# The norm of the differential heads in a hybrid attention backbone: per-query sums in a small tile, one root, and a spread by TensorE

## Chip, cores and metric

The kernel runs on one core of a Trainium2 chip. Its time is the device time of one execution in microseconds. Before the change three runs gave a median of 1594.83 us (1593.88 to 1594.98).

## The reference

Two layers are computed on 256 latent tokens and 256 context tokens of width 2048. One input projection feeds three groups of heads: MLA (6 heads), windowed attention (SWA, 6 query heads) and differential attention (4 heads). One output projection takes their gated results. The part that the change touches is the norm over the 128 features of each differential head:

```
oc_x = block_sweep(lambda qb: diff_attend(qb, kc_all, vc_all, lam), qc_x)
yc_x = (rms_norm(oc_x, dif_out_gain[l]) * (1.0 - lam_init)).reshape(b, s, DIFF_WIDTH)
...
y_x = jnp.concatenate([ya_x * silu(mla_gate), yb_x * silu(swa_gate), yc_x * silu(dif_gate)], axis=-1) @ w_out[l]
```

So for each query and each head a sum of 128 squares is made, a reciprocal root is taken of it, and the 128 features of that query and head are multiplied by it. In layer 0 this is done for 512 queries (context included), in layer 1, the last, for the 256 latent ones.

## The kernel before

**Projections.** All products are made in single precision from pieces: a weight block is loaded by a DMA on SP's queue (tile raw), rounded by ScalarE to its high part (hi, L237), and the low part is made by VectorE (lo, L238). TensorE then issues three matmuls for each slice of 128 rows and each token tile: L272 (hi), L273 (lo), L274 (hi, with the low part of the tokens).

**Order of the work.** Each layer runs MLA, then the differential heads (`dif`), then the windowed heads (`swa`), then the output projection. `run(main, side, ...)` issues a list of projection matmuls (main) and weaves in other steps (side) by their costs. A scheduler then orders the instructions of each engine, and each engine works through its own list in that order. The main lists of `swa` start while the last steps of `dif` are still under way. `swa` projects queries in two halves (sq0 and sq1, 384 columns each) and then keys and values. When a token tile of a half is done, ScalarE copies it out of PSUM into a tile sqraw (L1059). The copy, the tile p of the attention steps and the rotary tile rp share one ring of six 128x512 buffers, `stg`. On a latent tile the rotary turn is made by two POOL operations (L640, L641 into rp) and two VectorE operations (L642 on sqraw, L643 adds rp). In layer 0 the `swa` run also carries a fill: a 2048-column adaLN product, whose 1 MB weight tiles wada (16 of them) are loaded on SP's queue between the raw loads (L528) and multiplied by TensorE (L537).

**The norm of the differential heads** is in `C(h, s)` of `dif`, once for each head h and each set s of 256 queries: 8 times in layer 0, 4 times in layer 1. The output o lies in PSUM as features by queries. ScalarE squares it (L1210, tile dn), VectorE applies the gain and the gate (L1211, into oT), and TensorE multiplies by a 128x128 block of ones (L1213), so that each of the 128 rows holds the sums of all 256 queries. The root is taken of the whole 128x256 block: two operations of VectorE (L159, L160), then 13 of POOL (L163, and three rounds of L165 to L168), and a POOL multiply (L1215).

**MLA's keys.** For each pair of heads, `rope_k` (POOL, L944, one operation of 128x512 that writes the rotary part of kn) stands in the side list ahead of `nope_k(0)` and `nope_k(2)` (VectorE L946 and ScalarE L949 write the other part). TensorE transposes kn after that (L197). There are six such places.

Of the kernel before, what the change touches and what calls it, by code (L numbers as in the profile page):

```python
# [10 lines left out]
F32 = mybir.dt.float32  # L11
# [3 lines left out]
AF = mybir.ActivationFunctionType  # L15
ALU = mybir.AluOpType
# [3 lines left out]
P = 128  # L20
# [16 lines left out]
C_ONE = 128  # L37
# [76 lines left out]
class Builder:  # L114
# [36 lines left out]
    def bank_t(self):  # L151
        return self.psx.tile([P, 512], F32, tag="x", name="x")

    def rsqrt(self, y, ss, scale, tmp=None, pool=False):

        v = self.nc.vector
        n = y.shape[-1]
        x, t = tmp if tmp is not None else (self.sm(n, "rx"), self.sm(n, "rt"))
        v.tensor_scalar(x, ss, scale, EPS, ALU.mult, ALU.add)  # L159
        v.tensor_scalar(y.bitcast(I32), x.bitcast(I32), -0.5, 1597463007.0, ALU.mult, ALU.add)  # L160
        if pool:
            v = self.nc.gpsimd
            v.tensor_scalar(x, x, -0.5, 0.0, ALU.mult, ALU.add)  # L163
            for _ in range(3):
                v.tensor_tensor(t, y, y, ALU.mult)  # L165
                v.tensor_tensor(t, t, x, ALU.mult)
                v.tensor_scalar(t, t, 1.0, 1.5, ALU.mult, ALU.add)
                v.tensor_tensor(y, y, t, ALU.mult)  # L168
            return
        v.tensor_scalar(x, x, -0.5, None, ALU.mult)  # L170
        for _ in range(3):
            v.tensor_tensor(t, y, y, ALU.mult)
            v.tensor_tensor(t, t, x, ALU.mult)
            v.scalar_tensor_tensor(y, t, 1.5, y, ALU.add, ALU.mult)
# [179 lines left out]
class Layer:  # L354
# [528 lines left out]
    def mla(self, ip):  # L883
        B, nc, tc = self.B, self.B.nc, self.B.tc
        qt, T = self.qt, self.tok
        nq = len(qt)
# [12 lines left out]
        scale = (P + 64) ** -0.5  # L899
# [3 lines left out]
        for p in range(3):  # L903
# [3 lines left out]
            v = [vv[:, 0], vv[:, 1]]  # L907
# [52 lines left out]
            def nope_k(t):  # L960
                def f():
                    ps = B.bank_t().rearrange("p (h q) -> p h q", h=2)
                    for h in range(2):
                        for i in range(2):
                            B.tr(ps[:, h, i * P:(i + 1) * P], kn[:, t + i, h])
                    B.split(kT[0][:, 0:2, t * P:(t + 2) * P], kT[1][:, 0:2, t * P:(t + 2) * P], ps)
                return f

            def prep_q(s):
                def f():  # L970
                    q = [mp.tile([P, 3, 256], F32R, tag=f"qT{i}", name="qT") for i in range(2)]
                    ql = mp.tile([P, 2, 256], F32R, tag="qTl", name="qTl")
                    qTs[s] = q + [ql]
                    ps = B.bank_t().rearrange("p (h q) -> p h q", h=2)
                    pr = B.bank_t()[:, :256]
                    for i in range(2):
                        for h in range(2):
                            B.tr(ps[:, h, i * P:(i + 1) * P], qr[:, 2 * s + i, h])
                        B.tr(pr[:, i * P:(i + 1) * P], qr[:, 2 * s + i, 2])

                    g = self.prm[:, 73:74]
                    nc.scalar.activation(q[0][:, 0:2], ps, AF.Copy, scale=g)
                    nc.vector.scalar_tensor_tensor(q[1][:, 0:2], ps, g, q[0][:, 0:2].bitcast(F32), ALU.mult, ALU.subtract)
                    B.repeat((q[0][:, 2], q[1][:, 2]), (ql[:, 0], ql[:, 1]), pr)
                return f
# [18 lines left out]
                o = self.pv(lambda k: (v[0][:, 2 * s + k, hh], v[1][:, 2 * s + k, hh]), 4 if s == 0 else 2)  # L1004
                self.gated(h, s, o)
            side = [(300.0, prep_q1, None), (300.0, prep_k1, None)]
            side += [(440.0, f, None) for f in (rope_k, nope_k(0), nope_k(2))]
            pre = {(2 * p, s, 0): [(660.0, prep_q(s), None)] for s in range(nq // 2)}
            side += self.units([(h, s, i) for s in (0, 1) for h in (2 * p, 2 * p + 1) for i in (0, 1)], A, C, pre)
            B.run(gate(p + 1) if p < 2 else [], side, lead=4000.0)  # L1010
# [3 lines left out]
    def swa(self, gp):  # L1014
        B, nc = self.B, self.B.nc
        qt, T = self.qt, self.tok
        nq = len(qt)
# [3 lines left out]
        fill = Fill(self.in_swa, lambda: gp.tile([P, 2048], F32, tag=("skT", "sqT1")[next(turn) % 2], name="wada"), 1) if self.in_swa else None  # L1021
        kT = []
        v = [gp.tile([P, 4, 2, P], F32R, name=f"sv{i}") for i in range(2)]
# [5 lines left out]
        scale = P ** -0.5  # L1029
# [35 lines left out]
        m1 = B.gemm_tok(self.b["sq", 0], nh, nl, NK, qt, 384, ev_q(0))  # L1065
        m2 = B.gemm_tok(self.b["sq", 1], nh, nl, NK, qt, 384, ev_q(1))
        m = m1 + m2 + m0
        B.run(m, fill=(fill, 8, 4, len(m) - 1) if fill else None)

        def prep_q1():  # L1070
            n = 6 * nq
# [5 lines left out]
        def prep_t(g, t):  # L1077
            def f():
                if t == 0:
                    qTs[g] = [gp.tile([P, (3 * T, nT)[i]], F32R, tag=f"sqT{i}", name="sqT")[:, :3 * T].rearrange("p (k t) -> p k t", k=3) for i in range(2)]  # L1080
                ps = B.bank_t().rearrange("p (k q) -> p k q", k=4)[:, :3]
                for i in range(3):
                    B.tr(ps[:, i], qr[g][:, t, i])
                ts_ = slice(t * P, (t + 1) * P)
                B.split(qTs[g][0][:, :, ts_], qTs[g][1][:, :, ts_], ps)
            return f
# [23 lines left out]
        side = self.units([(h, s, i) for h in range(6) for s in (0, 1) for i in (0, 1)], A, C, {(3, 0, 0): [(330.0, prep_t(1, t), None) for t in qt]})  # L1110
        n = len(side) // 3
# [4 lines left out]
    def dif(self, gp):  # L1116
        B, nc = self.B, self.B.nc
        qt, T = self.qt, self.tok
        nq = len(qt)
# [4 lines left out]
        fill = Fill(self.in_dif, lambda: gp.tile([P, 2048], F32, tag=f"dkT{next(turn) % 2}", name="wada"), 1)  # L1124
        kT = []
        v = [gp.tile([P, 4, 512], F32R, name=f"dv{i}") for i in range(2)]
# [4 lines left out]
        scale = 64 ** -0.5  # L1131
# [41 lines left out]
        def prep_q1():  # L1173
            n = 8 * nq
            B.rsqrt(rq[:, 0, :n], ssq[:, :n], 1.0 / 64)
            nc.vector.tensor_scalar(rq[:, 0, :n], rq[:, 0, :n], scale, None, ALU.mult)
            nc.vector.tensor_scalar(rq[:, 1, :n], rq[:, 0, :n], -1.0, None, ALU.mult)
        qTs = {}

        def prep_t(h):  # L1180
            def f():

                qTs[h] = q = [gp.tile([P, T], F32R, tag=f"dqT{i}", name="dqT", bufs=2 - i // 2) for i in range(4)]
                ps = B.bank_t()
                for t in qt:
                    B.tr(ps[:, t * P:(t + 1) * P], qr[:, t, h * P:(h + 1) * P])
                B.repeat(q[:2], q[2:], ps[:, :T])
            return f
# [17 lines left out]
        def C(h, s):  # L1206
            o = self.pv(lambda k: (v[0][:, 2 * s + k, h * P:(h + 1) * P], v[1][:, 2 * s + k, h * P:(h + 1) * P]), 4 if s == 0 else 2)
            d = self.oT[h + 12][:, 256 * s:256 * s + 256]
            x = gp.tile([P, 3, 256], F32, tag="dn", name="dn", bufs=2)
            nc.scalar.activation(x[:, 0], o[:, :256], AF.Square)  # L1210
            nc.vector.scalar_tensor_tensor(d, o[:, :256], self.ogain, d, ALU.mult, ALU.mult)  # L1211
            sv = B.bank_t()
            nc.tensor.matmul(sv[:, :256], B.cst[:, C_ONE:C_ONE + P], x[:, 0], start=True, stop=True)  # L1213
            B.rsqrt(x[:, 0], sv[:, :256], 1.0 / P, (x[:, 1], x[:, 2]), pool=True)
            nc.gpsimd.tensor_tensor(d, d, x[:, 0], ALU.mult)  # L1215

        def gate(p):
            return B.gemm_feat(self.b["dg", p], nh, nl, T, 2, self.gate_fin([12 + 2 * p, 13 + 2 * p]))
        prep_q1()
        prep_t(0)()  # L1220
        B.run(gate(0))
        side = self.units([(h, s, i) for h in range(4) for s in (0, 1) for i in (0, 1)], A, C, {(h, 0, 0): [(440.0, prep_t(h), None)] for h in (1, 2, 3)}, depth=1)
        n = len(side) // 2
        B.run(gate(1), side[:n], lead=2000.0)
        B.run([], side[n:])

    def w_out(self, hp, sink_fn, pools, side=()):

# [182 lines left out]
```

## Time and profile before

| | before |
|---|---|
| median of 3 runs | 1594.83 us |
| profiled execution: its time | 1594.01 us |
| its span | 1592.2 us |
| PE busy | 1523.0 us |
| VectorE (DVE) busy | 921.2 us |
| ScalarE (ACT) busy | 702.3 us |
| POOL busy | 267.8 us |

The span is the time from the first to the last recorded instruction, 1.8 us less than that execution's own time. Busy times are summed over instructions of an engine. A matmul's record overlaps the next one's, so where a stream of matmuls is timed, the distance between starts is what counts. "Clock" is the clock granted to TensorE as a share of 2.4 GHz: 0.50 is 1.2 GHz.

### The profile page before, as it was taken

What the parts mean: (1) busy time and instruction counts of PE and PEld (TensorE: products, weight loads), DVE (VectorE), ACT (ScalarE), POOL (GpSimd) and SP (SyncE); (2) the same over time, 40 slices, a digit from 0 to 9 for tenths busy, and PEclk for the clock granted to TensorE, in tenths of its full rate; (3) what the DMA queues carried; (4) which work ended last, traced back from release to release, by engine and by line L of the source; (5) the groups of instructions that cost most, each with busy time, mean ns of one, the idle gap of its engine ahead of it and who ended that gap; (6) DMA issues with size and microseconds to landing.
All of it is one profiled execution on the core that took longest, in us unless ns stands there. A gap on an engine that the chain in (4) does not pass through costs nothing.

```text
span 1592.2 us, 22493 instructions
## 1 busy us (share of the span) xinstructions
PE 1523.0 (96%) x8213; PEld 1222.9 (77%) x8213; DVE 921.2 (58%) x1922; ACT 702.3 (44%) x1561; POOL 267.8 (17%) x429
## 2 busy tenths in 40 slices
PE   5999999999999987999999999999999999799998
PEld 2667888877778875878887777798876778789887
DVE  3445677642546971345853325958762389638854
ACT  4223556642244651334742224637752356426632
POOL 1002110100111892000010001020100133800100
PEclk9999999999999998999999999999999999999999
DMA  9997312246543125742146667554337662433374
GB/s 334 346 331 201 91 59 60 72 166 231 195 137 95 36 100 199 274 132 80 54 166 220 229 231 259 154 138 138 93 121 253 234 207 82 130 118 120 120 239 144
DMA packets 146769, 262.33 MB, mean 165 GB/s; under 512 B 9531, under 2 KB 90698, under 8 KB 137954
## 3 DMA queue, kind: packets, MB, share of 16 engines
q1 hardware_dynamic: 139056, 246.07, 46.4%
q0 software_dynamic: 2880, 6.39, 1.9%
q10 hardware_dynamic: 4722, 8.43, 1.6%
q8 instruction: 65, 1.06, 0.3%
q14 instruction: 46, 0.38, 0.1%
HBM read 256.63 MB, written 4.22 MB: 164 GB/s over the span
## 4 chain that ended last, share of the span: by engine, by line
PE 48%; DVE 5%; issue 3%; POOL 2%; ACT 2%; DMA 1%; DVEq 0%; POOLq 0%; ACTq 0%
PE g L272 11%; PE g L273 11%; PE g L274 11%; PE x L537 3%; PE x L663 2%; PE g L303 2%; PE g L302 2%; PE g L301 2%; PE x L197 2%; DVE lo L238 2%; ACT hi L237 1%; PE x L706 1%; PE x L707 1%; PE x L708 1%; DMA xres<-in_ctx_dram 0%
## 5 line engine op out<-in xcount | busy, mean ns | idle before, releaser
L238 DVE TENSOR_TENSOR lo<-raw,hi 128x1024 fp32r<-128x1024 f32 (+2 forms) x264 | 313.2, 1188 | 426.6 <-ACT hi L237 421.2
L237 ACT CAST hi<-raw 128x1024 fp32r<-128x1024 f32 (+2 forms) x264 | 266.8, 1011 | 528.9 <-PE g L274 442.8
L273 PE MATMUL g<-lo,nh 128*128 128x512 f32 (+2 forms) x1216 | 460.7, 379 | 14.6 <-DVE lo L238 14.5
L272 PE MATMUL g<-hi,nh 128*128 128x512 f32 (+2 forms) x1216 | 462.7, 382 | 7.6 <-ACT sqraw L1059 5.9
L274 PE MATMUL g<-hi,nl 128*128 128x512 f32 (+2 forms) x1216 | 458.9, 378 | 4.5 <-DVE nl L629 4.5
L272 PEld LDWEIGHTS g<-hi,nh 128*128 128x128 f32 x1216 | 230.6, 190 | 70.4 <-issue 19.3
L273 PEld LDWEIGHTS g<-lo,nh 128*128 128x128 f32 x1216 | 231.2, 190 | 53.7 <-DVE lo L238 17.7
L274 PEld LDWEIGHTS g<-hi,nl 128*128 128x128 f32 x1216 | 230.9, 190 | 45.2 <-DVE nl L629 6.8
L301 PE MATMUL g<-nh,hi 128*128 128x512 f32 (+1 forms) x512 | 175.9, 343 | 0.0
L303 PE MATMUL g<-nh,lo 128*128 128x512 f32 (+1 forms) x512 | 173.4, 339 | 0.0
L302 PE MATMUL g<-nl,hi 128*128 128x512 f32 (+1 forms) x512 | 172.7, 337 | 0.0
L303 PEld LDWEIGHTS g<-nh,lo 128*128 128x128 f32 x512 | 97.0, 189 | 10.2
L301 PEld LDWEIGHTS g<-nh,hi 128*128 128x128 f32 x512 | 97.1, 190 | 9.2 <-DVE v L178 0.4
L302 PEld LDWEIGHTS g<-nl,hi 128*128 128x128 f32 x512 | 97.1, 190 | 9.2
L766 POOL TENSOR_TENSOR oT<-oT,yo 128x256 f32<-128x256 f32 x36 | 28.3, 787 | 333.7 <-ACT yo L764 331.2
L674 DVE TENSOR_REDUCE sst<-x 128x1 f32<-128x512 f32 (+1 forms) x120 | 70.1, 596 | 17.8 <-PE x L663 16.8
L537 PE MATMUL x<-wada,sT 128*32 128x512 f32 x512 | 63.7, 607 | 0.0
L177 ACT CAST pth<-x 128x512 fp32r<-128x512 f32 (+1 forms) x96 | 48.6, 516 | 33.1 <-PE x L197 32.8
L178 DVE TENSOR_TENSOR ptl<-x,pth 128x512 fp32r<-128x512 f32 (+1 forms) x96 | 56.8, 596 | 9.2 <-ACT pth L177 6.0
L197 PE MATMUL x<-cst,p 128*128 128x128 f32 x320 | 51.2, 275 | 3.6 <-DVE p L1203 2.5
L197 PEld LDWEIGHTS x<-cst,p 128*128 128x128 f32 x320 | 37.2, 140 | 15.4 <-issue 6.3
L495 PE MATMUL x<-ar,sT 128*32 128x512 f32 x256 | 35.5, 619 | 11.2 <-DMA ar<-in_w_ada_dram 11.2
(331 smaller groups left out, 2165.2 us busy)
## 6 DMA issues: line engine op xcount, KB each, us to landing
raw<-in_w_in_dram SPq DMA_DIRECT2D x144, 512.0 KB, 3.6
wada<-in_w_ada_dram SPq DMA_DIRECT2D x64, 1024.0 KB, 6.5
raw<-in_w_out_dram SPq DMA_DIRECT2D x72, 512.0 KB, 4.0
ar<-in_w_ada_dram SPq DMA_DIRECT2D x128, 256.0 KB, 6.1
raw<-in_w_in_dram SPq DMA_DIRECT2D x32, 384.0 KB, 3.2
raw<-in_w_in_dram SPq DMA_DIRECT2D x16, 320.0 KB, 3.5
raw<-in_mla_w_uq_dram SPq DMA_DIRECT2D x12, 384.0 KB, 3.1
raw<-in_mla_w_ukv_dram SPq DMA_DIRECT2D x6, 512.0 KB, 3.4
```

What stands on the lines that cost most here:

```text
L178: self.nc.vector.tensor_tensor(lo, src, hi.bitcast(F32), ALU.subtract)
L197: self.nc.tensor.transpose(dst, src, self.ident[:src.shape[0], :src.shape[0]])
L237: nc.scalar.copy(b.hi, raw)
L238: nc.vector.tensor_tensor(b.lo, raw, b.hi.bitcast(F32), ALU.subtract)
L272: mm(ps, xh[:, k, ts_], b.hi[:, kk], start=(i == 0), stop=False)
L273: mm(ps, xh[:, k, ts_], b.lo[:, kk], start=False, stop=False)
L274: mm(ps, xl[:, k, ts_], b.hi[:, kk], start=False, stop=(i == nk - 1))
L301: mm(ps, b.hi[:, kk, fs], xh[:, k, :tok], start=(k == 0), stop=False)
L302: mm(ps, b.hi[:, kk, fs], xl[:, k, :tok], start=False, stop=False)
L303: mm(ps, b.lo[:, kk, fs], xh[:, k, :tok], start=False, stop=(k == NK - 1))
L537: nc.tensor.matmul(st["ps"][32 * j:32 * j + 32], B.sT[:, i, :], st[i][:, 512 * j:512 * j + 512], start=(i == 0), stop=(i == NK - 1), skip_ ...
L674: nc.vector.tensor_reduce(mx, s[:, :n], AX.X, ALU.max)
```

## The change

The change keeps of the norm only the square in `C`. TensorE takes the sum over the features with the squares as the stationary operand and two columns of ones as the moving one, twice for each (h, s), so that the sum of a query lands on its own partition. ScalarE copies one of the columns into a small tile dss of 128 x (tile, head). A new function `dif_norm` takes one root of the whole of dss on VectorE (12 operations of 128x16, in layer 1 of 128x8). Then, for each head, TensorE multiplies a root broadcast over 128 columns by the identity for each tile of tokens, which puts the roots of the queries along the columns on all partitions, and VectorE multiplies the head's oT by that. These five steps are side items of the `swa` run, allowed from its main items 6, 9, 12, 15 and 18 on. The root by POOL is gone. In MLA's side list rope_k is put after the two nope_k.

```
-    def rsqrt(self, y, ss, scale, tmp=None, pool=False):
+    def rsqrt(self, y, ss, scale):
...
-        if pool:
-            v = self.nc.gpsimd
-            v.tensor_scalar(x, x, -0.5, 0.0, ALU.mult, ALU.add)
-            for _ in range(3):
-                v.tensor_tensor(t, y, y, ALU.mult)
-                v.tensor_tensor(t, t, x, ALU.mult)
-                v.tensor_scalar(t, t, 1.0, 1.5, ALU.mult, ALU.add)
-                v.tensor_tensor(y, y, t, ALU.mult)
-            return
...
-            side += [(440.0, f, None) for f in (rope_k, nope_k(0), nope_k(2))]
+            side += [(440.0, f, None) for f in (nope_k(0), nope_k(2), rope_k)]
...
-        B.run(m, fill=(fill, 8, 4, len(m) - 1) if fill else None)
+        B.run(m, fill=(fill, 8, 4, len(m) - 1) if fill else None, side=[(100.0, f, 6 + 3 * i) for i, f in enumerate(self.dif_norm())])
...
-            x = gp.tile([P, 3, 256], F32, tag="dn", name="dn", bufs=2)
-            nc.scalar.activation(x[:, 0], o[:, :256], AF.Square)
+            x = gp.tile([P, 256], F32, tag="dn", name="dn", bufs=2)
+            nc.scalar.activation(x, o[:, :256], AF.Square)
             nc.vector.scalar_tensor_tensor(d, o[:, :256], self.ogain, d, ALU.mult, ALU.mult)
             sv = B.bank_t()
-            nc.tensor.matmul(sv[:, :256], B.cst[:, C_ONE:C_ONE + P], x[:, 0], start=True, stop=True)
-            B.rsqrt(x[:, 0], sv[:, :256], 1.0 / P, (x[:, 1], x[:, 2]), pool=True)
-            nc.gpsimd.tensor_tensor(d, d, x[:, 0], ALU.mult)
+            for i in range(2):
+                nc.tensor.matmul(sv[:, 2 * i:2 * i + 2], x[:, i * P:(i + 1) * P], B.cst[:, C_ONE:C_ONE + 2], start=True, stop=True)
+            nc.scalar.copy(self.dss[:, 2 * s:2 * s + 2, h:h + 1], sv[:, :4].rearrange("p (i c) -> p i c", i=2)[:, :, 0:1])
...
+    def dif_norm(self):
...
+        def scale():
+            B.rsqrt(r[:, :nq].rearrange("p t h -> p (t h)"), self.dss[:, :nq].rearrange("p t h -> p (t h)"), 1.0 / P)
+
+        def head(h):
+            def f():
+                t_ = B.bank_t()
+                for t in range(nq):
+                    nc.tensor.matmul(t_[:, t * P:(t + 1) * P], r[:, t, h:h + 1].to_broadcast([P, P]), B.ident, start=True, stop=True)
+                d = self.oT[h + 12][:, :self.tok]
+                nc.vector.tensor_tensor(d, d, t_[:, :self.tok], ALU.mult)
+            return f
+        return [scale] + [head(h) for h in range(4)]
```

Three places show how the order of instructions moves. The numbers of lines after the first few are nine lower in the changed kernel (L640 becomes L631, L238 becomes L229).

The first is POOL in layer 0, from the end of the differential heads into the `swa` projection; rp is the rotary tile of a query half, Tsq a table, dn the tile of the norm. Before:

```order
L640 TENSOR_TENSOR rp_5698<-sqraw,Tsq 128x3x64
L167 TENSOR_SCALAR dn<-dn 128x256
L641 TENSOR_TENSOR rp_5698<-sqraw,Tsq 128x3x64
L168 TENSOR_TENSOR dn<-dn 128x256
L165 TENSOR_TENSOR dn<-dn 128x256
L166 TENSOR_TENSOR dn<-dn 128x256
L640 TENSOR_TENSOR rp_5715<-sqraw,Tsq 128x3x64
L167 TENSOR_SCALAR dn<-dn 128x256
L641 TENSOR_TENSOR rp_5715<-sqraw,Tsq 128x3x64
L168 TENSOR_TENSOR dn<-dn 128x256
L1215 TENSOR_TENSOR oT_3394<-oT_3394,dn 128x256
```

With the change, POOL at the same place (gsq is the gain that is folded into the table ahead of the projection):

```order
L438 TENSOR_TENSOR Tsq<-Tsq,gsq 128x64
L439 TENSOR_TENSOR Tsq<-Tsq,gsq 128x64
L631 TENSOR_TENSOR rp_5608<-sqraw,Tsq 128x3x64
L632 TENSOR_TENSOR rp_5608<-sqraw,Tsq 128x3x64
L631 TENSOR_TENSOR rp_5625<-sqraw,Tsq 128x3x64
L632 TENSOR_TENSOR rp_5625<-sqraw,Tsq 128x3x64
```

The rotary operations no longer stand between and behind those of the norm; nothing but the tables stands ahead of them.

The second is VectorE in layer 1, from the last gain of a differential head (into oT) on; lo is the low part of a weight block, sqr the turned query tile. Before:

```order
L1211 SCALAR_TENSOR_TENSOR oT_11016<-x,og,oT_11016 128x256
L159 TENSOR_SCALAR dn<-x 128x256
L160 TENSOR_SCALAR dn<-dn 128x256
L238 TENSOR_TENSOR lo<-raw,hi 128x768 x3
L642 TENSOR_TENSOR sqr_12621<-sqraw,Tsq 128x384 x2
L643 TENSOR_TENSOR sqr_12621<-sqr_12621,rp_12769 128x384
L643 TENSOR_TENSOR sqr_12621<-sqr_12621,rp_12786 128x384
L238 TENSOR_TENSOR lo<-raw,hi 128x768 x3
```

With the change (dss is the tile of sums, dr the roots, rx and rt temporaries):

```order
L1202 SCALAR_TENSOR_TENSOR oT_10944<-x,og,oT_10944 128x256
L159 TENSOR_SCALAR rx<-dss 128x8
L633 TENSOR_TENSOR sqr_12494<-sqraw,Tsq 128x384
L160 TENSOR_SCALAR dr<-rx 128x8
L633 TENSOR_TENSOR sqr_12494<-sqraw,Tsq 128x384
L161 TENSOR_SCALAR rx<-rx 128x8
L163 TENSOR_TENSOR rt<-dr 128x8
L634 TENSOR_TENSOR sqr_12494<-sqr_12494,rp_12657 128x384
L164 TENSOR_TENSOR rt<-rt,rx 128x8
L634 TENSOR_TENSOR sqr_12494<-sqr_12494,rp_12678 128x384
L165 SCALAR_TENSOR_TENSOR dr<-rt,dr 128x8
L229 TENSOR_TENSOR lo<-raw,hi 128x768
```

The rotary part now stands before three low parts that stood ahead of it, and the root's small operations lie between.

The third is SP's queue in layer 0 at the start of the `swa` projection; raw 128x2x384 are the query weights, wada the fill's. Before:

```order
L222 DMA raw<-in_w_in_dram 128x4x256 x8
L222 DMA raw<-in_w_in_dram 128x2x384 x13
L528 DMA wada<-in_w_ada_dram 128x2048 x8
L222 DMA raw<-in_w_in_dram 128x2x384 x3
L528 DMA wada<-in_w_ada_dram 128x2048 x2
```

With the change:

```order
L213 DMA raw<-in_w_in_dram 128x4x256 x8
L213 DMA raw<-in_w_in_dram 128x2x384 x12
L519 DMA wada<-in_w_ada_dram 128x2048 x6
L213 DMA raw<-in_w_in_dram 128x2x384
L519 DMA wada<-in_w_ada_dram 128x2048 x2
```

The fill's loads stand one query block earlier in the queue, and the last raw loads are spread between them. On TensorE 64 projection matmuls stood between the last sum over features and the fill's first matmul; with the change there are 29.

## Rows read from the trace of the kernel before

**Rows 1.** The page, part 1: busy time of each engine.

```profile
PE 1523.0 (96%) x8213; PEld 1222.9 (77%) x8213; DVE 921.2 (58%) x1922; ACT 702.3 (44%) x1561; POOL 267.8 (17%) x429
```

**Rows 2.** Windows: stretch, length, busy time of each engine, clock, DMA share, GB/s.

```profile
515.00:590.00 75.00, 71.07 (x396) 59.56 (x395) 68.92 (x160) 41.96 (x98) 64.14 (x92) 1.00 0.16 48
...
600.00:605.00 5.00, 2.61 (x7) 2.10 (x7) 1.47 (x2) 0.88 (x4) 4.84 (x9) 0.50 0.00 0
605.00:610.00 5.00, 1.94 (x8) 1.34 (x12) 3.87 (x5) 1.31 (x6) 1.17 (x2) 0.50 0.00 0
610.00:615.00 5.00, 5.00 (x29) 2.79 (x21) 0.00 (x0) 0.00 (x0) 0.00 (x0) 0.76 0.49 157
1330.00:1365.00 35.00, 31.39 (x177) 26.22 (x176) 33.96 (x75) 22.97 (x51) 21.48 (x30) 1.00 0.20 57
...
1385.00:1390.00 5.00, 4.68 (x15) 4.68 (x16) 2.73 (x3) 0.76 (x1) 4.59 (x6) 0.50 0.69 218
```

**Rows 3.** Waits of PE: us in total, times, longest us.

```profile
PE g L273 <- DVE lo L238: 14.5, 7, 6.4
...
PE x L197 <- POOL kn L944: 6.9, 6, 1.3
PE g L272 <- ACT sqraw L1059: 5.9, 1, 5.9
```

**Rows 4.** Timeline of PE at two places; in brackets idle time before.

```profile
601.27 0.69 PE L272 MATMUL g<-hi,nh 128*128 128x384 f32 x1 [5.91 <-ACT sqraw L1059]
...
608.06 0.69 PE L273 MATMUL g<-lo,nh 128*128 128x384 f32 x1 [4.18 <-DVE lo L238]
...
1377.17 0.33 PE L273 MATMUL g<-lo,nh 128*128 128x384 f32 x1
...
1378.56 0.34 PE L272 MATMUL g<-hi,nh 128*128 128x384 f32 x1
1385.32 0.69 PE L273 MATMUL g<-lo,nh 128*128 128x384 f32 x1 [6.42 <-DVE lo L238]
```

**Rows 5.** Timeline of ACT and DVE around the rotary operations.

```profile
600.74 0.48 ACT L1059 COPY sqraw<-g 128x384 f32<-128x384 f32 x1 [6.69 <-POOL rp L641]
...
1382.91 0.95 DVE L643 TENSOR_TENSOR sqr<-sqr,rp 128x384 f32<-128x384 f32 x1 [3.58 <-POOL rp L641]
```

**Rows 6.** Timeline of one pair of MLA's heads, layer 1, all engines.

```profile
1093.21 0.17 DVE L174 SCALAR_TENSOR_TENSOR rk<-rt,rk 128x8 f32<-128x8 f32 x1
...
1093.41 0.69 DVE L946 TENSOR_TENSOR kn<-kn,rk 128x512 f32<-128x512 f32 x1
1093.45 1.55 POOL L944 TENSOR_TENSOR kn<-krr,rk 128x512 f32<-128x512 f32 x1 [9.73 <-DVE rk L174]
...
1093.47 1.28 ACT L949 ACTIVATE kn<-kn,rk 128x128 f32<-128x128 f32 x4
...
1095.06 1.53 PE L197 MATMUL x<-cst,kn 128*128 128x128 f32 x12 [1.32 <-POOL kn L944]
...
1096.42 0.60 PE L197 MATMUL x<-cst,qr 128*128 128x128 f32 x4
```

**Rows 7.** Timeline of PE: four matmuls of two columns and what follows.

```profile
45.76 0.95 PE L504 MATMUL x<-cst,adas 128*128 128x2 f32 x8
46.57 0.63 PE L197 MATMUL x<-cst,h 128*128 128x128 f32 x4
```

**Rows 8.** The instructions of L1213: ns min/median/max.

```profile
L1213 PE MATMUL x<-dn,cst x24: 377/379/483, 514.7 to 1367.7; 128*128 128x256 f32 x24
```

**Rows 9.** The instructions of L643: ns min/median/max.

```profile
L643 DVE TENSOR_TENSOR sqr<-sqr,rp x8: 547/842/1066, 600.7 to 1398.6; 128x384 f32<-128x384 f32 x8
```

**Rows 10.** Tile wada, 585 to 660 us: its 12 loads on SP's queue.

```profile
DMA to landing us min/median/max: 4.8/4.9/6.8
```

**Rows 11.** Timeline of PE: two of the fill's batches in layer 0.

```profile
614.38 1.07 PE L537 MATMUL x<-wada,sT 128*32 128x512 f32 x8
...
617.86 1.07 PE L537 MATMUL x<-wada,sT 128*32 128x512 f32 x8
```

More of the change, by code (lines that the diff above doesn't have):

```diff
@@ L152, in bank_t @@
         return self.psx.tile([P, 512], F32, tag="x", name="x")
-    def rsqrt(self, y, ss, scale, tmp=None, pool=False):
+    def rsqrt(self, y, ss, scale):
         v = self.nc.vector
         n = y.shape[-1]
-        x, t = tmp if tmp is not None else (self.sm(n, "rx"), self.sm(n, "rt"))
+        x, t = self.sm(n, "rx"), self.sm(n, "rt")
         v.tensor_scalar(x, ss, scale, EPS, ALU.mult, ALU.add)
         v.tensor_scalar(y.bitcast(I32), x.bitcast(I32), -0.5, 1597463007.0, ALU.mult, ALU.add)
-        if pool:
-            v = self.nc.gpsimd
-            v.tensor_scalar(x, x, -0.5, 0.0, ALU.mult, ALU.add)
-            for _ in range(3):
-                v.tensor_tensor(t, y, y, ALU.mult)
-                v.tensor_tensor(t, t, x, ALU.mult)
-                v.tensor_scalar(t, t, 1.0, 1.5, ALU.mult, ALU.add)
-                v.tensor_tensor(y, y, t, ALU.mult)
-            return
         v.tensor_scalar(x, x, -0.5, None, ALU.mult)
@@ L1208, in C @@
             d = self.oT[h + 12][:, 256 * s:256 * s + 256]
-            x = gp.tile([P, 3, 256], F32, tag="dn", name="dn", bufs=2)
-            nc.scalar.activation(x[:, 0], o[:, :256], AF.Square)
+            x = gp.tile([P, 256], F32, tag="dn", name="dn", bufs=2)
+            nc.scalar.activation(x, o[:, :256], AF.Square)
             nc.vector.scalar_tensor_tensor(d, o[:, :256], self.ogain, d, ALU.mult, ALU.mult)
             sv = B.bank_t()
-            nc.tensor.matmul(sv[:, :256], B.cst[:, C_ONE:C_ONE + P], x[:, 0], start=True, stop=True)
-            B.rsqrt(x[:, 0], sv[:, :256], 1.0 / P, (x[:, 1], x[:, 2]), pool=True)
-            nc.gpsimd.tensor_tensor(d, d, x[:, 0], ALU.mult)
+            for i in range(2):
+                nc.tensor.matmul(sv[:, 2 * i:2 * i + 2], x[:, i * P:(i + 1) * P], B.cst[:, C_ONE:C_ONE + 2], start=True, stop=True)
+            nc.scalar.copy(self.dss[:, 2 * s:2 * s + 2, h:h + 1], sv[:, :4].rearrange("p (i c) -> p i c", i=2)[:, :, 0:1])
         def gate(p):
             return B.gemm_feat(self.b["dg", p], nh, nl, T, 2, self.gate_fin([12 + 2 * p, 13 + 2 * p]))
+        self.dss = B.lp.tile([P, 4, 4], F32, tag="dss", name="dss", bufs=2)
         prep_q1()
@@ L1225, in dif @@
         B.run([], side[n:])
+    def dif_norm(self):
+        B, nc = self.B, self.B.nc
+        nq = len(self.qt)
+        r = B.lp.tile([P, 4, 4], F32, tag="dr", name="dr")
+        def scale():
[9 more added lines that the diff above has]
+        return [scale] + [head(h) for h in range(4)]
     def w_out(self, hp, sink_fn, pools, side=()):
```

## Prediction

> **What bounds the kernel now.** I read the busy times first, then PE's waits, then the windows around the longest waits, then the timelines of the engines that release them. The reader is to see that TensorE is the bound: it is busy for 1523.0 of 1592.2 us and no other engine passes 921.2 [rows 1]. POOL's whole 267.8 us count only where something waits for them. So a gain must come out of PE's idle time (69 us in all), out of work taken off PE, or out of stretches in which PE ran at a lower clock.
>
> PE's waits show where such idle time lies near the change [rows 3]. The longest wait for a low part is 6.4 us; it stands in layer 1 just before 1385.32, and one of 4.18 us in layer 0 before 608.06 [rows 4]. The wait for sqraw is 5.91 us, before 601.27 [rows 4]. These three stand at the change of `dif` to `swa` in both layers, and both chains end at POOL. ScalarE's copy at 600.74 had stood 6.69 us until POOL had written rp, and VectorE's L643 in layer 1 stood 3.58 us for the same [rows 5]. ScalarE needs the copy's place in the ring of staging tiles, which a rotary tile still holds. VectorE works in order, so the low parts listed behind L643 come late, and PE with them. POOL is late with the rotary operations because it is still taking roots: it was busy 64.14 of the 75 us from 515 to 590, and 4.84 of 5 from 600 to 605 [rows 2]. The order of POOL shows what the rotary operations stand among: rounds of the root.
>
> After these waits the clock is down. It is 0.50 of full speed from 600 to 610 and 0.76 from 610 to 615, and 0.50 from 1385 to 1390 [rows 2]; that is 1.2 GHz instead of 2.4, after PE had been nearly idle for some 6 us.
>
> **Layer 0, the change of groups.** The change takes 14 operations per head and set off POOL, 112 in layer 0, so the rotary operations follow their sqraw at once. The waits of 5.91 and 4.18 us go: 10.1 us. The lower clock costs the busy time by its missing share: 2.61 x 0.50 + 1.94 x 0.50 + 5.00 x 0.24 = 3.5 us [rows 2]; I take 3.0, since PE may still meet a short hole. What replaces the wait? From the first sqraw on, the next low part that PE lacks stands behind two L642 and two L643 (each about 0.84, the median of L643 [rows 9]), two gain operations and one head multiply (taken as 0.8 each): 0.5 for the copy + 3.4 + 2.4 + 1.0 for the low part itself = 7.3 us. In that time PE has 42 projection matmuls at 0.174 us (eight steps from 1377.17 to 1378.56 [rows 4]), 7.3 us, one or two heads' matmuls, and the fill's first batch of 1.07 [rows 11]. That is just covered, so I take no wait here; the other end is 2 us.
>
> **Layer 1, the change of groups.** Here VectorE's order has the rotary part ahead of the next low part. Behind the last gain come five of the root's small operations (0.17 each, 0.2 apart [rows 6]), two L642, two L643 and the low part: 0.5 + 1.0 + 3.4 + 1.2 = 6.1 us. By the order PE has 27 projection matmuls whose low parts are ready, 27 x 0.174 = 4.7 us. So a wait of 1.4 us takes the place of the one of 6.42: 5.0 gained. The ends are 0 (all gone) and 3 (the second L643 waits for POOL's four rotary operations). The clock at 0.50 cost 4.68 x 0.50 = 2.3 us up to 1390 [rows 2] and a little after; I take 2.5, as a wait of 1.4 is short beside the holes after which the clock fell.
>
> **The differential phase itself.** From 515 to 590 PE was idle for 75.00 - 71.07 = 3.9 us and from 1330 to 1365 for 35.00 - 31.39 = 3.6, while VectorE was busy for 68.92 and 33.96 us of them [rows 2]. VectorE is the limit there. The change takes two operations of 128x256 per head and set from it, in the chain, and POOL's company. VectorE's L643 of one shape took between 547 and 1066 ns [rows 9]; the slow one is beside a busy POOL. I take half of the idle time, 2.0 + 1.8 = 3.8 us, between the ends nothing (the chain through ScalarE's square and copy stays) and all 7.5. The Trainium skill, GPSIMD Engine Reference, section Specifications, says that POOL shares its SBUF interfaces with VectorE and that VectorE's operations with two SBUF inputs contend for them. L643 is of that kind and its two levels agree; by that rule all of VectorE's work here speeds up, and the sum would be 1566.
>
> **MLA's keys.** At each of six places PE waits for L944 [rows 3]. At one, L944 runs from 1093.45 to 1095.00, and twelve transposes follow at 1095.06 and end 1.36 later, when the next begin at 1096.42 [rows 6]: 0.113 each. VectorE's part was ready at 1094.10 and ScalarE's at 1094.75. With the rotary part last, four transposes run from 1094.15, four from 1094.81 and four to 1095.72: 0.7 earlier. Six times this is 4.2 us. The ends are 2 (the scheduler leaves a copy in between) and 6.9, the whole wait.
>
> **What is added to PE.** The sums: two matmuls of two columns for each head and set. Four such in a row took from 45.76 to 46.57, 0.20 each [rows 7], so 0.40 for a pair; L1213 has two records of 0.38 that overlap [rows 8]. I take no difference. The spread over columns: 16 matmuls in layer 0 and 8 in layer 1. No such operation is in the trace. It is of the same single precision as L504 with 128 columns instead of 2, so 0.20 is its lower end; half of L1213 (half its columns), 0.38 at most, its upper. I take 0.20, because the transposes of the same shape stand 0.113 apart [rows 6] and two passes of that are 0.23. So 24 x 0.20 = 4.8 us; at the upper end 9.1. The head multiplies (VectorE, 128x512, four in layer 0) and the root lie beside projection matmuls and cost nothing, unless as counted above. Twelve small copies of ScalarE lie in `dif`, where it was busy for 41.96 of 75 us [rows 2].
>
> **The sum.** Layer 0: 10.1 + 3.0 + 2.0 = 15.1. Layer 1: 5.0 + 2.5 + 1.8 = 9.3. MLA: 4.2. Together 28.6, less 4.8 is 23.8. From the profiled execution's 1594.0 us (0.8 below the median) this gives **1570**.
>
> **Rivals.**
> One wait stays: **1578** (1574 to 1586). In layer 1, if VectorE stands at its second L643 or the low part comes later than counted, the wait stays near 6 and the clock falls again: 5.0 + 2.5 back. Or the fill's first wait in layer 0: its loads now issue behind fewer raw loads, and PE wants them 35 matmuls (6 us) earlier. Landing took 4.9 us [rows 10]. The order on SP speaks for it, since a raw load that waits for a low part's place is still ahead of them.
>
> The differential phase loses all its idle time: **1566** (1560 to 1568). L643's two levels speak for it; against it that PE waits there also follow ScalarE.
>
> Nothing to be had: **1593**. If ScalarE's copy and VectorE's low parts were held by something other than POOL (the raw loads, say), both waits stay, and MLA's 4.2 and the new matmuls cancel. All releasers named above speak against it.
>
> Slower: the fill starves PE. A batch comes every 3.48 us (614.38 to 617.86 [rows 11]) into the place of the batch before last, so it may take 2 x 3.48 - 1.07 = 5.9 us from issue; each microsecond of landing above this is paid eight times. Landing took 4.9 at the median and 6.8 at most [rows 10]. With the raw loads now between the fill's loads, a landing of 9.5 us would cost 8 x 3.6 = 29 us and give **1599**; the deciding point is a landing of 8.9 us, where 24 us are eaten.
>
> **How the numbers follow.** Forecast 0.55, one wait stays 0.22, the whole phase relieved 0.13, nothing 0.05, starved fill 0.05. The forecast's own ends (new matmuls to 9.1, MLA to 2) reach 1576, the whole phase to about 1561. A range of 1561 to 1584 leaves out some 0.14: both bad cases and the ends. A measurement here tells about 0.2% (3 us) from no change. Faster by more than that: 0.55 + 0.22 + 0.13 and a little of the rest = 0.91; within it 0.05; slower 0.04.
>
> **What would show it.** In the changed trace: no wait of PE above 3 us between the last head's sums and the third query block in layer 0, ScalarE's sqraw copies within 1 us of PE's last matmul; a clock of 1.00 through both changes of group; in layer 1 one wait for a low part of about 1.4 us; PE's waits for kn near zero; the new head matmuls 0.2 us apart; PE's idle time in `dif` halved. The prediction is wrong if a low part waits more than 4 us in either layer, if PE waits at the fill's first batch, or if the heads' matmuls wait for the root on VectorE.

## The result, and the profile after

The changed kernel takes 1559.78 us (median of 4 runs, 1558.94 to 1560.57) against 1594.9 (1593.88 to 1595.42): a ratio of 0.978 with a 95% interval of 0.9764 to 0.9797. That is 35 us less, where 24 were forecast, and 1.2 us below the forecast range (1561 to 1584). The page's busy times (the row that answers to [rows 1]):

```profile
PE 1517.1 (97%) x8285; PEld 1225.4 (79%) x8285; DVE 904.8 (58%) x1930; ACT 701.7 (45%) x1573; POOL 147.5 (9%) x261
```

The span fell by 34.5 us, from 1592.2 to 1557.7, PE's busy time by 5.9, so 28.6 us of PE's idle time went. POOL lost 120 us. The waits of PE that answer to [rows 3] (us in total, times, longest):

```profile
PE x L486 <- DMA ar<-in_w_ada_dram: 11.7, 5, 9.9
PE x L188 <- DVE cth L1302: 6.6, 1, 6.6
...
PE g L264 <- DVE lo L229: 2.1, 3, 1.0
...
PE x L188 <- DVE kn L937: 0.7, 3, 0.3
```

The two longest lie in the first 140 us of the kernel, which the change does not touch. Of the waits named in the prediction, the one for low parts went from 14.5 to 2.1 us in all, the one for kn from 6.9 to 0.7, and the one for sqraw is gone. The windows of the changed kernel's same stretches (columns as in [rows 2]):

```profile
512.90:581.00 68.10, 67.92 (x411) 60.82 (x412) 58.32 (x156) 42.71 (x104) 0.11 (x1) 1.00 0.23 74
581.00:586.00 5.00, 5.00 (x34) 3.91 (x33) 4.41 (x8) 3.99 (x22) 2.87 (x4) 1.00 0.54 180
586.00:591.00 5.00, 5.00 (x32) 2.83 (x32) 1.52 (x3) 1.58 (x7) 0.00 (x0) 1.00 0.90 336
...
1307.00:1343.00 36.00, 35.84 (x220) 33.01 (x218) 33.31 (x75) 28.12 (x71) 3.72 (x4) 1.00 0.33 96
1343.00:1348.00 5.00, 5.00 (x33) 4.51 (x33) 3.40 (x12) 1.42 (x4) 0.00 (x0) 1.00 0.80 253
1348.00:1353.00 5.00, 4.88 (x30) 4.59 (x29) 4.49 (x12) 1.67 (x2) 0.00 (x0) 1.00 0.48 146
```

The first and the fourth are the differential phase of layer 0 and 1. PE is idle for 0.18 and 0.16 us there, where it was idle for 3.9 and 3.6 [rows 2]; VectorE is busy for 86% of the window in layer 0 (58.32 of 68.10 us) instead of 92% (68.92 of 75.00), and in layer 1 still for 93% (33.31 of 36.00) instead of 97%. At the changes of group, in the other rows, PE is full but for 0.12 us and the clock stays at 1.00. Where the time went, stage by stage, from the first rows of each kind in the two timelines (us, differences taken before rounding):

| stage | before | after | difference |
|---|---|---|---|
| start to first differential scores, layer 0 | 499.3 | 497.2 | -2.0 |
| from there to the first copy of a windowed key tile, layer 0 | 195.9 | 178.3 | -17.6 |
| from there to the first differential scores, layer 1 | 620.5 | 617.4 | -3.1 |
| from there to the last copy of a windowed key tile, layer 1 | 122.0 | 109.8 | -12.2 |
| from there to the end of the span | 154.5 | 155.0 | +0.5 |

The second and fourth rows hold the norm (29.8 us), the first and third MLA's order (5.1). The tests below name these the two differential stages.

### The profile page after: what moved, and what is told of

It reads as the page before. It is cut to its first block, busy times and chain, and to the rows that moved or that the text cites. A ratio compares the mean times of both kernels' runs of the same rounds, so it can differ in the third digit from the quotient of the medians.

```text
span 1557.7 us, 22477 instructions
## 1 busy us (share of the span) xinstructions
PE 1517.1 (97%) x8285; PEld 1225.4 (79%) x8285; DVE 904.8 (58%) x1930; ACT 701.7 (45%) x1573; POOL 147.5 (9%) x261
## 4 chain that ended last, share of the span: by engine, by line
PE 81%; DVE 7%; issue 4%; ACT 4%; DMA 3%; POOL 1%; SPq 0%; ACTq 0%; DVEq 0%; POOLq 0%
PE g L263 16%; PE g L265 16%; PE g L264 16%; PE x L188 4%; PE x L654 4%; PE g L292 4%; PE g L294 4%; PE g L293 4%; PE x L528 4%; DVE lo L229 2%; PE x L486 2%; ACT hi L228 1%; PE x L697 1%; DMA ar<-in_w_ada_dram 1%; PE x L698 1%
## 5 line engine op out<-in xcount | busy, mean ns | idle before, releaser
L229 DVE TENSOR_TENSOR lo<-raw,hi 128x1024 fp32r<-128x1024 f32 (+2 forms) x264 | 308.4, 1168 | 415.7 <-ACT hi L228 412.2
```

The lines of the kernel that those rows point to most:

```text
L229: nc.vector.tensor_tensor(b.lo, raw, b.hi.bitcast(F32), ALU.subtract)
```

## The experiments

Beside these experiments the kernel before was timed again, at medians of 1593.1 to 1593.7 us where it had taken 1594.9. The changed kernel was not, so a difference from its 1559.78 us is uncertain by 1 to 2 us.

Two theories were set against each other for what the forecast had missed, the differential phase. Theory P: a busy POOL slows VectorE, the limit there. Theory V: VectorE is the limit and lost two operations for each head and set.

**The two parts apart.** The kernel before with MLA's new order alone, and the changed kernel with the old one:

```
-            side += [(440.0, f, None) for f in (rope_k, nope_k(0), nope_k(2))]
+            side += [(440.0, f, None) for f in (nope_k(0), nope_k(2), rope_k)]
```

> The kernel before, with nothing changed but MLA's side list (rotary part of the keys behind the two other parts). Theory of the prediction: 0.7 us at each of six places, 4.2 us, so 1590.7. Read from the stage lengths of the changed kernel's trace: 4.8 us, so 1590.1. Rival, that the time saved in MLA is lost again at a later wait when the rest is unchanged: 1594 to 1595.

> The changed kernel with MLA's side list in its old order. If the two parts are independent: 1559.8 + 4.2 to 4.8, so 1564 to 1564.6. If they share a gain (the same idle time counted twice): under 1562, with MLA alone bringing more than its share.

Measured: 1589.58 us against 1593.72 for the order alone, 0.9971 (0.9959 to 0.9982), 4.1 us less; and 1564.06 for the norm alone, 0.9813 (0.9799 to 0.9828), 4.3 us more than the changed kernel. So the parts are independent within the uncertainty, and MLA's order is worth what was forecast. One pair of heads in the changed kernel, PE's timeline (the rows that answer to [rows 6]):

```profile
1073.96 1.55 PE L188 MATMUL x<-cst,kn 128*128 128x128 f32 x12 [0.16 <-DVE kn L937]
1075.35 0.60 PE L188 MATMUL x<-cst,qr 128*128 128x128 f32 x4
```

The twelve transposes start 0.16 us after PE was free instead of 1.32, and take 1.39 instead of 1.36: the rotary part no longer holds them up.

**POOL's load put back.** The changed kernel with POOL's old 14 operations after each head and set, on spare parts of dn whose results nobody reads, and the same after heads 0 and 1 alone (`h < 2`):

```
+            if h < 4:
+                u, w = y[:, 1], y[:, 2]
+                g = nc.gpsimd
+                g.tensor_scalar(u, x, 0.0, 0.5, ALU.mult, ALU.add)
+                for _ in range(3):
+                    g.tensor_tensor(w, u, u, ALU.mult)
+                    g.tensor_tensor(w, w, u, ALU.mult)
+                    g.tensor_scalar(w, w, 0.0, 1.0, ALU.mult, ALU.add)
+                    g.tensor_tensor(u, u, w, ALU.mult)
+                g.tensor_tensor(w, u, w, ALU.mult)
```

> The changed kernel with the old load put back on POOL alone: after each head and set POOL runs 14 operations of 128x256 on spare parts of the tile dn, whose results nobody reads. VectorE's two operations of 128x256 stay away. Theory P (POOL's load makes both the waits at the change of groups and VectorE's slowness in the differential phase): nearly all of the norm's gain goes, about 1560 + 30 = 1590 or a little less. Theory V (the differential phase sped up because VectorE lost its two operations): only the waits and the lower clock behind them return, 10 + 6.4 + 6.3 = 23 us, about 1582.

> The changed kernel with POOL's old load put back after heads 0 and 1 alone (4 of 8 head-and-set steps in layer 0, 2 of 4 in layer 1), results unread; POOL is done long before the rotary operations of the windowed heads. Theory P (a busy POOL slows VectorE and with it PE in the differential phase): VectorE's operations slow down while POOL runs, and half of the differential phase's share returns, 3 to 4 us: 1563 to 1564. Theory V (VectorE's own two operations made that share): at most 1 us, under 1561, and VectorE's durations as in the changed kernel.

Measured with all of it: 1584.53 us, 0.9943 (0.9928 to 0.9959) of before, between the two forecasts. PE's waits show both effects (us in total, times, longest):

```profile
PE g L263 <- ACT sqraw L1050: 10.4, 1, 10.4
...
PE x L1244 <- DVE dr L165: 2.8, 1, 2.8
...
PE x L1207 <- ACT dn L1202: 1.8, 4, 0.6
```

The wait for sqraw is back, 10.4 us in one piece, with POOL's work as the only thing added. In layer 0 the differential stage takes 197.1 us, more than before the change (195.9), with the spread's 3.3 us in it; in layer 1 114.4, where low parts hardly wait and PE stands 2.8 us at a heads' matmul for the root instead. VectorE's operations between 512 and 581 us in this kernel (count, busy, mean ns):

```profile
L229 DVE TENSOR_TENSOR lo<-raw,hi 128x768 fp32r<-128x768 f32 x8 | 9.2, 1149 | 0.5 <-ACT hi L228 0.5
...
L1194 DVE SCALAR_TENSOR_TENSOR p<-p,sst 128x512 f32<-128x512 f32 x6 | 5.9, 988 | 0.1
...
L169 DVE TENSOR_TENSOR ptl<-x,pth 128x512 fp32r<-128x512 f32 x6 | 4.1, 685 | 0.5 <-ACT pth L168 0.3
```

and the same groups of the changed kernel in the same stretch:

```profile
L229 DVE TENSOR_TENSOR lo<-raw,hi 128x768 fp32r<-128x768 f32 x9 | 8.6, 951 | 0.8 <-ACT hi L228 0.8
...
L1194 DVE SCALAR_TENSOR_TENSOR p<-p,sst 128x512 f32<-128x512 f32 x6 | 4.5, 744 | 0.1
L169 DVE TENSOR_TENSOR ptl<-x,pth 128x512 fp32r<-128x512 f32 x6 | 4.1, 691 | 0.9 <-ACT pth L168 0.8
```

The low parts (two inputs in SBUF) take 951 ns on average with POOL still and 1149 with POOL busy, the difference of the two probabilities 744 and 988; the low part of a transposed tile, whose first input is in PSUM, takes 691 and 685. The Trainium skill, GPSIMD Engine Reference, section Specifications, says that VectorE's operations with two SBUF inputs contend with POOL, and these rows agree with it. So a part of VectorE's work speeds up, and not all of it, as the prediction has it.

With POOL's load after the first two heads only: 1563.44 us (1563.12 to 1564.23), 3.7 more than the changed kernel. PE has no wait for sqraw there, and VectorE and ScalarE wait for none of POOL's added operations, so this is POOL's company alone, at half its dose: 2.5 us in layer 0's differential stage and 1.3 in layer 1's. The low parts of the same stretch take longer here too:

```profile
L229 DVE TENSOR_TENSOR lo<-raw,hi 128x768 fp32r<-128x768 f32 x8 | 8.2, 1026 | 0.0
```

Theory P holds for that much.

**VectorE's load put back.**

```
+            nc.vector.tensor_scalar(y[:, 1], o[:, :256], 0.0, 1.0, ALU.mult, ALU.add)
+            nc.vector.tensor_scalar(y[:, 2], y[:, 1], 0.5, 1.0, ALU.mult, ALU.add)
```

> The changed kernel with two operations of 128x256 put back on VectorE alone after each head and set (results unread, the first reading PSUM as the old one did). Theory V: the differential phase's share returns, 5 to 7 us: 1565 to 1567. Theory P: VectorE has room without POOL's company, at most 2 us: under 1562.

Measured: 1563.49 us (1560.83 to 1564.38), 3.7 more: below what theory V asks for, above what P alone allows. In the profiled run it is 1.8 us in layer 0's differential stage and 2.3 in layer 1's. VectorE's other operations keep their short times in it (the same window):

```profile
L229 DVE TENSOR_TENSOR lo<-raw,hi 128x768 fp32r<-128x768 f32 x9 | 8.6, 953 | 2.8 <-ACT hi L228 2.6
...
L1194 DVE SCALAR_TENSOR_TENSOR p<-p,sst 128x512 f32<-128x512 f32 x6 | 4.5, 745 | 0.0
```

But the 1.8 us in layer 0 do not lie in the differential phase. They are one wait of PE behind it, for a weight tile of the fill:

```profile
PE x L528 <- DMA wada<-in_w_ada_dram: 1.9, 1, 1.9
```

A wait of this kind (1.6 us) also stands in the profile of MLA's order alone, where the norm is that of the kernel before, so it does not need VectorE's load. The windows of the two differential phases with POOL's whole load, with half of it and with VectorE's load (columns as in [rows 2]; those of layer 1 start some 14 us behind its first scores, as in the changed kernel):

```profile
512.90:581.00 68.10, 65.60 (x381) 55.33 (x381) 63.56 (x142) 40.40 (x99) 58.98 (x83) 1.00 0.17 47
1326.50:1362.50 36.00, 35.18 (x212) 31.39 (x211) 35.36 (x74) 27.36 (x70) 27.32 (x35) 1.00 0.31 88
```

```profile
512.90:581.00 68.10, 66.57 (x397) 58.00 (x397) 61.38 (x147) 41.02 (x100) 39.47 (x55) 1.00 0.20 59
1309.20:1345.20 36.00, 35.08 (x213) 31.52 (x212) 35.38 (x74) 27.57 (x70) 24.45 (x32) 1.00 0.32 89
```

```profile
512.90:581.00 68.10, 67.85 (x411) 60.58 (x410) 58.79 (x157) 43.65 (x110) 1.71 (x3) 1.00 0.20 55
1309.10:1345.10 36.00, 34.49 (x212) 30.67 (x211) 34.33 (x85) 25.26 (x64) 1.28 (x2) 1.00 0.29 81
```

PE is idle for 2.50, 1.53 and 0.25 us in layer 0, where the changed kernel has 0.18, and for 0.82, 0.92 and 1.51 in layer 1, where it has 0.16. So POOL's company acts in both layers, and in layer 0 it brings back most of the idle time alone; VectorE's two operations are shown to count in layer 1 only. Twice the half dose of POOL's company is 7.6 us (an estimate, as if the effect grew with the load), and VectorE's operations make 2.3 in layer 1: 9.9 us. The runs of the last one spread over 3.5 us, so its share is uncertain by about 2.

**The waits without the rest.** The kernel before, with POOL's roots, and only the rotary operations of the windowed queries moved to VectorE:

```
+        e = nc.vector if key == "sq" else nc.gpsimd
-        nc.gpsimd.tensor_tensor(t2[:, :, :h], x[:, :, h:], T[:, t, 1, :h].unsqueeze(1).to_broadcast([P, nh, h]), ALU.mult)
-        nc.gpsimd.tensor_tensor(t2[:, :, h:], x[:, :, :h], T[:, t, 1, h:].unsqueeze(1).to_broadcast([P, nh, h]), ALU.mult)
+        e.tensor_tensor(t2[:, :, :h], x[:, :, h:], T[:, t, 1, :h].unsqueeze(1).to_broadcast([P, nh, h]), ALU.mult)
+        e.tensor_tensor(t2[:, :, h:], x[:, :, :h], T[:, t, 1, h:].unsqueeze(1).to_broadcast([P, nh, h]), ALU.mult)
```

> The kernel before, with the rotary operations of the windowed queries moved from POOL to VectorE and nothing else changed: POOL's roots stay, but nothing on the way from sqraw waits for POOL. Theory of the waits (POOL's order makes the waits at both changes of group): the waits of 5.9, 4.2 and 6.4 us go with the lower clock behind them, VectorE gets 4 x 0.5 us per layer, so 20 to 22 us less than before: 1573 to 1576. Rival, that VectorE, slowed by POOL, is late with the low parts anyway: 1585 or more.

Measured: 1574.84 us, 0.9882 (0.9866 to 0.9899), 18.9 us less than before. Two of PE's waits and three windows of it (columns as in [rows 2]):

```profile
PE x L197 <- POOL kn L945: 6.9, 6, 1.3
...
PE g L273 <- DVE lo L238: 5.9, 7, 2.0
```

```profile
515.00:590.00 75.00, 71.04 (x396) 59.56 (x396) 68.97 (x160) 41.92 (x97) 64.06 (x92) 1.00 0.17 48
590.00:600.00 10.00, 7.98 (x45) 6.78 (x47) 10.00 (x13) 6.25 (x29) 9.84 (x12) 0.96 0.64 249
600.00:605.00 5.00, 5.00 (x29) 3.08 (x21) 0.98 (x1) 0.00 (x0) 4.51 (x7) 0.74 0.57 187
```

The wait for sqraw is gone, the longest for a low part is 2.0 us, and the differential phase is as it was: 71.04 us of PE in 75, as in [rows 2]. This separates the two gains: the waits came from POOL's order, and taking them away leaves the phase alone. 10.2 us came out of layer 0's differential stage and 8.5 out of layer 1's, a little short of the expectation: in layer 0 VectorE, busy for all of the 10 us from 590, is still 2.0 us late with a low part, and the clock is at 0.74 in the 5 us behind that wait.

**What the small tile and the delay are worth.** First, root, spread and multiply at once for each head and set, nothing deferred:

```
+            r = B.sm(2, "dr2")
+            B.rsqrt(r, sv[:, :4].rearrange("p (i c) -> p i c", i=2)[:, :, 0], 1.0 / P)
+            t_ = B.bank_t()
+            for i in range(2):
+                nc.tensor.matmul(t_[:, i * P:(i + 1) * P], r[:, i:i + 1].to_broadcast([P, P]), B.ident, start=True, stop=True)
+            nc.vector.tensor_tensor(d, d, t_[:, :256], ALU.mult)
```

> The changed kernel with root, spread and multiply made at once for each head and set (a root of 128x2, two heads' matmuls, one multiply of 128x256), nothing deferred to the next projections. If the small tile alone is what counts: VectorE gets 12 x 12 operations of 0.17 instead of 24, some of it covered, 1561 to 1565. If deferring counts: PE stands in its order at the heads' matmuls until VectorE's chain of 12 dependent operations (2.4 us and what is queued ahead of it) is through, 1568 to 1580.

Measured: 1574.47 us (1573.95 to 1574.99), 14.7 more than the changed kernel. PE's wait for the root in it:

```profile
PE x L1211 <- DVE dr L165: 5.4, 4, 3.4
```

The rest of the 14.7 is no single wait; 12.7 us of it lies in layer 0's differential stage, where VectorE now runs 96 small operations. Deferring, and with it one root for all heads in place of one for each head and set, is worth about as much as the waits and the clock at the change of groups in layer 0 (13.9). The two were not tried apart. Second, the kernel before with the wide root (128x256) on VectorE:

```
-            B.rsqrt(x[:, 0], sv[:, :256], 1.0 / P, (x[:, 1], x[:, 2]), pool=True)
-            nc.gpsimd.tensor_tensor(d, d, x[:, 0], ALU.mult)
+            B.rsqrt(x[:, 0], sv[:, :256], 1.0 / P, (x[:, 1], x[:, 2]))
+            nc.vector.tensor_tensor(d, d, x[:, 0], ALU.mult)
```

> The kernel before, with the 13 operations of POOL's root and the last multiply (all of 128x256) moved to VectorE; the sums stay spread over 128 rows. It tells how much of the gain needs the small tile. Theory (VectorE is the limit of the differential phase): 8 x 11 operations of some 0.3 us, 26 us in layer 0 and half as much in layer 1, come to an engine that was busy 69 of 75 us there; the waits for POOL go (23 us with the clock), POOL's company goes, and VectorE's load returns much of it or more: 1590 to 1605. Rival, that getting POOL out of the way is all that counts: 1565 to 1575.

Measured: 1591.81 us, 0.9986 (0.9976 to 0.9995) of before. Its windows over both differential phases:

```profile
515.00:600.00 85.00, 76.36 (x407) 65.05 (x406) 82.17 (x230) 44.23 (x109) 2.52 (x4) 0.96 0.15 43
...
1316.00:1370.00 54.00, 45.80 (x267) 38.93 (x265) 52.13 (x132) 30.70 (x67) 0.00 (x0) 0.97 0.24 66
```

POOL is out of the way, and VectorE is busy for 82.17 of 85 us; PE is idle for 8.6 and 8.2 us. Moving the wide root from POOL to VectorE brings next to nothing: it must also become small. No run tried the wide root on ScalarE.

**A cheaper spread.** A transpose of the same broadcast tile instead of the product with the identity:

```
-                    nc.tensor.matmul(t_[:, t * P:(t + 1) * P], r[:, t, h:h + 1].to_broadcast([P, P]), B.ident, start=True, stop=True)
+                    B.tr(t_[:, t * P:(t + 1) * P], r[:, t, h:h + 1].to_broadcast([P, P]))
```

> The changed kernel with the heads' matmuls against the identity replaced by transposes of the same broadcast tile (one record each instead of two). The trace has the heads' matmuls at 0.21 us each and transposes at about 0.11, so 24 x 0.10 = 2.4 us less: 1557.4. Rival, that the spread is hidden on PE or its price is set by the weight load: no change, 1559.8.

Measured: 1557.3 us (1556.38 to 1557.6), 2.5 less than the changed kernel, and its four runs all lie below that one's. The first head in layer 0 of the changed kernel, then of this one (PE's timeline):

```profile
583.77 1.16 PE L1233 MATMUL x<-cst,dr 128*128 128x128 f32 x8
584.68 0.42 PE L263 MATMUL g<-hi,nh 128*128 128x384 f32 x1
```

```profile
583.62 0.65 PE L188 MATMUL x<-cst,dr 128*128 128x128 f32 x4
584.02 0.42 PE L263 MATMUL g<-hi,nh 128*128 128x384 f32 x1
```

Four matmuls have eight records and take 0.91 us, four transposes four records and 0.40. Over all heads the spread takes 2.0 us by the distance of starts, where it took 4.8. The intervals of the two ratios to the kernel before overlap (0.9754 to 0.9781 here, 0.9764 to 0.9797 for the changed kernel), so the gain rests on these timelines as much as on the medians.

## Why the prediction was off

The direction and the places were right; the time fell just outside the range because one term, the differential phase, was mis-sized. The rival that pointed there was held at 0.13, and its 1566 us were short too, as it counted idle time alone.

- **Waits and clock in layer 0 (10.1 + 3.0):** right. PE's idle time in the stretch went from 10.1 us to nothing. The slower clock had cost 3.8, by the distance of starts above that at full clock: 2.9 for the projection matmuls between 600 and 615 us and 0.9 for the fill's first batch.
- **Wait and clock in layer 1 (5.0 + 2.5):** the new wait of 1.4 us did not come; 6.4 went, and the clock's 2.5 (the 17 matmuls from 1385.32 on, by the distance of starts). VectorE's timeline in the changed kernel, from the root on, shows why:

```profile
1346.12 0.17 DVE L159 TENSOR_SCALAR rx<-dss 128x8 f32<-128x8 f32 x1 [0.37 <-ACT dss L1207]
1346.20 0.56 DVE L633 TENSOR_TENSOR sqr<-sqraw,Tsq 128x384 f32<-128x384 f32 x1
...
1347.37 0.55 DVE L634 TENSOR_TENSOR sqr<-sqr,rp 128x384 f32<-128x384 f32 x1
1347.84 0.16 DVE L164 TENSOR_TENSOR rt<-rt,rx 128x8 f32<-128x8 f32 x1
...
1348.46 0.96 DVE L229 TENSOR_TENSOR lo<-raw,hi 128x768 fp32r<-128x768 f32 x1
```

From the first operation of the root to the end of the low part it is 3.3 us, where 5.6 were counted behind the copy. The price of L642 and L643 (0.84) was the median of eight L643, five of them beside a busy POOL; here they take 0.55, the low end in [rows 9]. The small operations take 0.08 of pitch when an unrelated one follows, not 0.2.
- **The differential phase (3.8): the step that failed.** "I take half of the idle time" was too little, and idle time itself too small a measure. The two differential stages fell by 29.8 us; taking off waits (16.5), clock (6.3) and adding back the spread (4.8) leaves 11.8. Of that 7.2 us was idle time in windows ([rows 2] against the rows above); the remaining 4.6 is by subtraction. PE's timelines agree with it: between the first scores and the last sums over features, beside the marked waits, the distances of starts exceed the medians of the same neighbours by 5.4 us before and 2.5 after in layer 0, and by 3.5 and 1.7 in layer 1. So matmuls also stood a little further apart without a wait being marked. The experiments give POOL's company 7.6 (twice the measured half) and VectorE's two operations 2.3, in layer 1; the other 2 us, in layer 0, stay open. POOL's company, which the prediction saw in L643's two levels and counted at half the idle time, was the main mechanism.
- **MLA (4.2):** 4.1 and 4.3 by the two experiments; the profiled executions show 5.1.
- **The spread (4.8):** 3.3 us in layer 0 and 1.5 in layer 1 by the distance of starts, 4.8. The multiplies and the root are hidden, as said.
- **The starved fill:** did not happen. The loads landed in 5.3 us at the median and 7.4 at most, a little later than in [rows 10], and PE had no wait for the tile wada (the 12 loads issued between 575 and 640 us):

```profile
DMA to landing us min/median/max: 4.8/5.3/7.4
```

The miss of 11 us is thus 8 from the differential phase, 1.4 from the wait that did not come, 0.8 from the clock and 1 from MLA in the profiled run.

## What to carry to other kernels

When a chain is taken off POOL, count three things apart: who waits behind it in POOL's order, how much faster VectorE's operations with two SBUF inputs become beside a still POOL, and what VectorE itself loses or gains. The price of a VectorE operation is not a median over the trace, but its time beside the POOL that the changed kernel will have. A root of sums belongs on the smallest tile that holds them, and can be made once, later, beside matmuls that don't need it.

## What was not expected of the hardware

The same VectorE operation took 951 or 1149 ns on average (128x768, two SBUF inputs) with POOL idle or busy, while one with a PSUM input stayed at 691 and 685. A chain of dependent small operations on VectorE stood 0.2 us apart [rows 6], and 0.08 apart from a following operation that did not depend on it. A transpose of a broadcast column did the spread in 0.10 us for the first head, where the matmul in single precision took 0.23. Behind one wait of 2.0 us (the rotary operations on VectorE) the granted clock was 0.74 over 5 us; behind the fill's wait of 1.9 us (VectorE's load put back) it stayed at 1.00. The prediction had counted no loss of clock behind a wait of 1.4 us, which no run tested.
